# Norm application on Trainium2: the column scale moved into VectorE's multiplication, the shift on ScalarE, GpSimd taken out

## The chip, the cores and the metric

The kernel runs on one core of a Trainium2 chip. A core has five engines that work side by side from queues of their own: TensorE (PE, matrix products), VectorE (DVE), ScalarE (ACT), GpSimd (POOL) and SyncE (SP, which here starts the transfers). The metric is the device time of one execution in microseconds, from the first instruction to the last.

## The reference

Two transformer blocks of depth 2 each, on 512 tokens (the first block with 256 context tokens beside them) of width 1024, in float32. What matters here are the norms between the matrix products:

```
def rms_norm(x, g):
    y = x * lax.rsqrt(jnp.mean(x * x, axis=-1, keepdims=True) + EPS)
    return y * g
def modulate(h, shift, scale):
    return h * (1.0 + scale) + shift
def layer_norm(x, g, b):
    mu = jnp.mean(x, axis=-1, keepdims=True)
    var = jnp.mean(jnp.square(x - mu), axis=-1, keepdims=True)
    return (x - mu) * lax.rsqrt(var + LN_EPS) * g + b
```

The first block applies the RMS norm with a shift and a scale ahead of w_in and of w_up, and adds each product to the residual that was there before the norm. The second block applies the layer norm after w_mix, w_mo and w_ff2, and its result is the next residual.

## The kernel before

Activations lie with the features on the partitions: eight tiles `xs[0..7]` of 128 features by 512 tokens (768 with the context). A product in full precision is three products of rounded numbers: each weight tile and each activation is split into a rounded high part and a low part, and TensorE adds up high x high, low x high and high x low. So a norm's output is a pair: `h[:, 0]` is the rounded value, and `h[:, 1]` is the residual, the unrounded value less the rounded one.

*Weights.* A transfer brings a weight tile `wf`; ScalarE rounds it to `wh` (L241), and an engine subtracts to get `wl` (L243; the names end in x for the second of two sets of buffers). That engine is GpSimd for the matrices in `POOL_SPLIT` (w_in, w_in2, w_mix, w_out), else VectorE, unless `split_on` names another one.

*Norms.* The scale and shift are columns, one number per feature and so per partition; the deviation `r` and the mean `mu` are tiles of one number per token. For each of the eight tiles a norm does: VectorE multiplies by `r` (L294, L358, L1460); ScalarE scales, shifts and rounds to `h[:, 0]` (L298, L362, L1465); GpSimd scales and shifts without rounding (L299, L366, L1469); VectorE subtracts for the residual (L300, L367, L1471). There are three places in the code. `rms_chunks` makes the first norm of the kernel, 768 columns wide. `norm_linear` holds the RMS norms that follow a product (w_out, w_down): the last products and the norm go in two pieces of columns, 512 and 256, or 256 and 256, so that the norm of one piece goes beside the products of the other. `res_norm` with `ln_feed`, `ln_late`, `ln_stats` and `ln_apply` does the same for the layer norms, in two halves of 256 columns. There `ln_apply` first subtracts the mean (L1456, tiles 0 to 4 on VectorE and 5 to 7 on GpSimd, by `LND`), and what GpSimd makes is written back to `xs` as the next residual; ScalarE does this in its place for tiles 0 and 4 (`AFA`, L1467), and for tiles 1, 3, 5, 7 in the last norm (`AFB`), which makes no `h`.

*The head.* While a half is normed, TensorE takes each finished `h` tile at once into the first products of the next matrix (the `head`: L1487 is w_mq's, L1507 w_in2's, L1067 w_up's, L1090 w_in's, L529 those of the first norm). At the two places in `LNC` (half 0 behind tile 7, half 1 behind tile 3) `res_norm` has the next weight tile split, and with `LNP` set this is put on GpSimd whatever the matrix.

*Order.* Code is issued tile by tile; a scheduler then orders each engine's queue ahead of time, and at run time an engine takes its queue strictly in order. What VectorE or ScalarE holds ahead of a tile's `h` therefore delays it, whatever else is ready.

## Time and profile before

| | us |
|---|---|
| median of 3 runs (lowest to highest) | 3614.79 (3611.59 to 3618.96) |
| the profiled execution | 3614.98 |
| its span in the profile | 3613.2 |
| TensorE busy | 3404.7 |
| VectorE busy | 2062.0 |
| ScalarE busy | 1616.5 |
| GpSimd busy | 764.6 |

The mean granted clock of TensorE over the span is 0.979 of full speed. A timeline row gives the start, the duration, the engine, the line, the operation, what is written and read, and how many instructions of this kind stand in a row; in brackets is how long the engine was idle before, and what released it. Where several stand in one row, the duration is that of all together.

### The profile page before, as it was taken

The page shows a single profiled execution, that of the slowest core. Times are in us where ns is not written, and L with a number is a line of the kernel's source. Part 1 is how long each engine was busy: PE and PEld are TensorE (multiplying, and loading weights), DVE is VectorE, ACT ScalarE, POOL GpSimd, SP SyncE. Part 2 cuts the span into 40 slices and gives each one's busy share as a digit, 9 for nine tenths or more (in the row PEclk, how much of TensorE's full clock was granted, in tenths as well). Part 3 has the DMA queues.
Part 4 walks back from the last instruction along what each step waited for, and adds up shares of the span by engine and source line. Part 5 has one row for each costly group of instructions (what it writes and reads, how often), then busy time and mean ns, then how long its engine had stood idle before and what let it go on. Part 6 is the DMA issues. An engine that isn't in the chain of part 4 may idle for free. (4 is left out here: it accounts for less than half of the span.)

```text
span 3613.2 us, 51613 instructions
## 1 busy us (share of the span) xinstructions
PE 3404.7 (94%) x19888; PEld 2864.2 (79%) x19888; DVE 2062.0 (57%) x4037; ACT 1616.5 (45%) x3239; POOL 764.6 (21%) x706
## 2 busy tenths in 40 slices
PE   7999999999998999899999999899998989999998
PEld 5777777888887778688887777788887877888887
DVE  5765537777445764455555774664446683664444
ACT  4876624222224766543335454543224455443323
POOL 3233232000004233320002315230005314340002
PEclk9999999999999999999999999999999999999999
DMA  6111252445122010323323242323232243303331
GB/s 210 32 44 60 71 203 89 134 150 188 53 62 68 27 59 32 99 74 100 94 86 94 76 141 73 117 71 99 99 93 79 65 129 98 128 30 111 99 99 59
DMA packets 118054, 333.71 MB, mean 92 GB/s; under 512 B 18736, under 2 KB 35632, under 8 KB 117168
## 3 DMA queue, kind: packets, MB, share of 16 engines
q1 hardware_dynamic: 117808, 330.41, 28.9%
q8 instruction: 157, 2.57, 0.3%
q14 instruction: 89, 0.73, 0.1%
HBM read 313.19 MB, written 17.18 MB: 91 GB/s over the span
## 5 line engine op out<-in xcount | busy, mean ns | idle before, releaser
L241 ACT CAST wh<-wf 128x1024 fp32r<-128x1024 f32 (+1 forms) x245 | 250.2, 1022 | 555.9 <-PE M L1570 254.2
L243 DVE TENSOR_TENSOR wl<-wf,wh 128x1024 fp32r<-128x1024 f32 (+1 forms) x168 | 196.9, 1172 | 258.0 <-ACT wh L241 257.9
L496 PE MATMUL M<-wh,h 128*128 128x256 f32 x1472 | 321.7, 294 | 7.4 <-ACT t_st L565 3.0
L243 POOL TENSOR_TENSOR wl<-wf,wh 128x1024 fp32r<-128x1024 f32 x77 | 185.0, 2406 | 651.1 <-ACT wh L241 616.8
L1106 PE MATMUL S<-h,wh 128*128 128x512 f32 x1008 | 268.4, 361 | 6.2 <-DVE y L1118 5.9
L241 ACT CAST whx<-wf 128x1024 fp32r<-128x1024 f32 (+2 forms) x211 | 210.5, 998 | 137.4 <-PE M L1570 61.4
L496 PEld LDWEIGHTS M<-wh,h 128*128 128x128 f32 x1472 | 245.7, 191 | 28.4 <-issue 21.8
L1106 PE MATMUL S<-h,whx 128*128 128x512 f32 x1008 | 265.0, 358 | 0.0
L243 DVE TENSOR_TENSOR wlx<-wf,whx 128x1024 fp32r<-128x1024 f32 (+2 forms) x168 | 199.4, 1187 | 39.0 <-ACT whx L241 38.2
L496 PE MATMUL M<-wl,h 128*128 128x256 f32 x736 | 210.4, 286 | 3.3 <-POOL wl L243 3.3
L1684 PE MATMUL T<-ident,P 128*128 128x128 f32 x1136 | 186.1, 282 | 18.6 <-POOL P L1676 5.3
L1106 PEld LDWEIGHTS S<-h,wh 128*128 128x128 f32 x1008 | 168.1, 190 | 38.1 <-ACT wh L241 3.9
L1106 PEld LDWEIGHTS S<-h,whx 128*128 128x128 f32 x1008 | 165.7, 188 | 29.3
L788 ACT COPY pT<-T 128x512 f32<-128x512 f32 (+1 forms) x280 | 156.5, 569 | 58.2 <-PE T L1684 47.7
L1684 PEld LDWEIGHTS T<-ident,P 128*128 128x128 f32 x1136 | 129.6, 142 | 53.8 <-POOL P L1676 12.4
L1116 DVE SCALAR_TENSOR_TENSOR y<-S,pp,y 128x511 f32<-128x511 f32 (+1 forms) x132 | 86.6, 657 | 143.8 <-ACT y L1113 143.7
L1113 ACT ACTIVATE y<-S,pp 128x768 f32<-128x768 f32 (+1 forms) x88 | 77.8, 886 | 187.7 <-PE S L1106 181.5
L1570 PE MATMUL S<-h,wh 128*128 128x512 f32 x480 | 158.1, 390 | 0.0
L1570 PE MATMUL S<-h,whx 128*128 128x512 f32 x480 | 157.5, 389 | 0.0
L1106 PE MATMUL S<-h,wl 128*128 128x512 f32 x504 | 154.7, 361 | 0.0
L1106 PE MATMUL S<-h,wlx 128*128 128x512 f32 x504 | 152.2, 356 | 0.0
L691 PE MATMUL S<-k,q 128*128 128x512 f32 (+1 forms) x576 | 142.6, 353 | 9.1 <-ACT P L750 4.2
(518 smaller groups left out, 9215.9 us busy)
## 6 DMA issues: line engine op xcount, KB each, us to landing
wf<-in_w_ff_dram SPq DMA_DIRECT2D x128, 512.0 KB, 3.4
wf<-in_w_up_dram SPq DMA_DIRECT2D x88, 512.0 KB, 3.5
wf<-in_w_in_dram SPq DMA_DIRECT2D x80, 512.0 KB, 3.5
af<-in_adaT_dram SPq DMA_DIRECT2D x56, 512.0 KB, 4.1
wf<-in_w_down_dram SPq DMA_DIRECT2D x48, 384.0 KB, 3.1
wf<-in_w_mkv_dram SPq DMA_DIRECT2D x32, 512.0 KB, 3.6
ak<-in_adaK_dram SPq DMA_DIRECT2D x16, 512.0 KB, 9.4
wf<-in_w_out_dram SPq DMA_DIRECT2D x16, 512.0 KB, 3.6
```

The lines of the kernel that those rows point to most:

```text
L241: self.nc.scalar.copy(hi, f)
L243: eng.tensor_sub(lo, f, hi.bitcast(F32))
L496: mm = self.nc.tensor.matmul(ps[:, :256], a, c, start=(n == 0), stop=(n == 23))
L691: self.nc.tensor.matmul(ps[:, a:b], lhs, r[:, a:b], start=(i == 0), stop=(i == n - 1))
L788: nc.scalar.copy(hl[:, :w], pT[:, :w])
L1106: nc.tensor.matmul(ps[:, s0:s1], a, hs[k][:, mj, s0:s1], start=(q == 0), stop=(q == 23))
L1113: nc.scalar.activation(y[:, :n], ps[:, :n], AF.Identity, scale=col(cw + 1), bias=col(cb))
L1116: nc.vector.scalar_tensor_tensor(y[:, s0 + 1:s1], ps[:, s0:s1 - 1], col(cw), y[:, s0 + 1:s1], op0=ALU.mult, op1=ALU.add)
L1570: self.nc.tensor.matmul(ps, w[k // 4][jw][:, k % 4, c * P:(c + 1) * P], hs[k][:, jm], start=(i == 0), stop=(i == 23))
L1684: self.nc.tensor.transpose(pT[:, n * P:(n + 1) * P], pt[:, j, (kp + i) * P:(kp + i + 1) * P], self.ident)
```

## The change

In all three places VectorE's multiplication now takes the scale column as well, `(x * scale) * r`, in one three-operand instruction; ScalarE adds the shift and rounds; VectorE makes the residual as `(x + shift) - h`, again in one instruction. GpSimd has no part in it. In `rms_chunks` the 768 columns become 512 and 256 on VectorE, as the scale differs for the context. In `ln_apply` all eight mean subtractions are VectorE's, the product is written in place (the temporary tile is gone), and since `xs` must then hold x + b, ScalarE adds it for all eight tiles: after the loop where `h` is made, in the loop in the last norm. `LNP` is 0, so that the splits at the places of `LNC` are VectorE's unless the matrix is in `POOL_SPLIT`. The constants `LND`, `AFA`, `AFB` and `NAF` are gone.

```diff
-LNP = 1
+LNP = 0
@@ rms_chunks
-            nc.vector.tensor_mul(t[:, :n], xs[m][:, :n], r[:, :n])
...
-                    nc.scalar.activation(h[:, 0, a:b], t[:, a:b], AF.Identity, scale=scale(m, v), bias=shift(m, v))
-                    nc.gpsimd.tensor_scalar(t[:, a:b], t[:, a:b], scale(m, v), shift(m, v), op0=ALU.mult, op1=ALU.add)
-            nc.vector.tensor_sub(h[:, 1, :n], t[:, :n], h[:, 0, :n].bitcast(F32))
+                    nc.vector.scalar_tensor_tensor(t[:, a:b], xs[m][:, a:b], scale(m, v), r[:, a:b], op0=ALU.mult, op1=ALU.mult)
+                    nc.scalar.activation(h[:, 0, a:b], t[:, a:b], AF.Identity, bias=shift(m, v))
+                    nc.vector.scalar_tensor_tensor(h[:, 1, a:b], t[:, a:b], shift(m, v), h[:, 0, a:b].bitcast(F32),
+                                                   op0=ALU.add, op1=ALU.subtract)
@@ norm_linear
-                nc.vector.tensor_mul(t, xs[m][:, a:b], r[:, a:b])
+                nc.vector.scalar_tensor_tensor(t, xs[m][:, a:b], scale(m, v), r[:, a:b], op0=ALU.mult, op1=ALU.mult)
...
-                self.behind = nc.scalar.activation(h[:, 0, a:b], t, AF.Identity, scale=scale(m, v), bias=shift(m, v))
...
-                    nc.gpsimd.tensor_scalar(t, t, scale(m, v), shift(m, v), op0=ALU.mult, op1=ALU.add)
-                self.behind_v = nc.vector.tensor_sub(h[:, 1, a:b], t, h[:, 0, a:b].bitcast(F32))
+                self.behind = nc.scalar.activation(h[:, 0, a:b], t, AF.Identity, bias=shift(m, v))
+                self.behind_v = nc.vector.scalar_tensor_tensor(h[:, 1, a:b], t, shift(m, v), h[:, 0, a:b].bitcast(F32),
+                                                               op0=ALU.add, op1=ALU.subtract)
@@ ln_apply
-            (nc.vector if m < LND else nc.gpsimd).tensor_sub(x, x, mu)
+            nc.vector.tensor_sub(x, x, mu)
...
-            nc.vector.tensor_mul(t, x, r)
+            nc.vector.scalar_tensor_tensor(x, x, g(m), r, op0=ALU.mult, op1=ALU.mult)
...
-                self.behind = nc.scalar.activation(h[:, 0, sl], t, AF.Identity, scale=g(m), bias=b(m))
-            if m in (AFA if hs is not None else AFB):
-                nc.scalar.activation(x, t, AF.Identity, scale=g(m), bias=b(m))
+                self.behind = nc.scalar.activation(h[:, 0, sl], x, AF.Identity, bias=b(m))
+                nc.vector.scalar_tensor_tensor(h[:, 1, sl], x, b(m), h[:, 0, sl].bitcast(F32), op0=ALU.add, op1=ALU.subtract)
             else:
-                nc.gpsimd.tensor_scalar(x, t, g(m), b(m), op0=ALU.mult, op1=ALU.add)
-            if hs is not None:
-                nc.vector.tensor_sub(h[:, 1, sl], x, h[:, 0, sl].bitcast(F32))
+                nc.scalar.activation(x, x, AF.Identity, bias=b(m))
             yield m
+        for m in range(KC) if hs is not None else ():
+            nc.scalar.activation(xs[m][:, sl], xs[m][:, sl], AF.Identity, bias=b(m))
```

Where `h` is made, ScalarE writes `xs` in 20 instructions before (two in each of ten halves) and in 80 after; in the last norm in 8 before and 16 after. VectorE makes the subtractions of the mean in 60 instructions before and 96 after.

VectorE's queue at the start of half 1 of the norm after w_mix in the first layer, before. L1456 subtracts the mean, L1444 makes the variance, L1460 multiplies into the temporary `pT`, L1471 makes the residual; `x2_0` to `x2_7` are the tiles, `score2` is the mean and `score3` the deviation:

```order
L1456 TENSOR_TENSOR x2_0_18102<-x2_0_18102,score2_21278 128x256
L1471 TENSOR_TENSOR h6_21649<-x2_6_18114,h6_21649 128x256
L1444 SCALAR_TENSOR_TENSOR score3_21279<-T_21580,score3_21279 128x256
L1456 TENSOR_TENSOR x2_1_18104<-x2_1_18104,score2_21278 128x256
L1471 TENSOR_TENSOR h7_21661<-x2_7_18116,h7_21661 128x256
L1456 TENSOR_TENSOR x2_2_18106<-x2_2_18106,score2_21278 128x256
L1456 TENSOR_TENSOR x2_3_18108<-x2_3_18108,score2_21278 128x256
L1456 TENSOR_TENSOR x2_4_18110<-x2_4_18110,score2_21278 128x256
L1460 TENSOR_TENSOR pT_21685<-x2_0_18102,score3_21279 128x256
L1460 TENSOR_TENSOR pT_21696<-x2_1_18104,score3_21279 128x256
L1460 TENSOR_TENSOR pT_21707<-x2_2_18106,score3_21279 128x256
L1471 TENSOR_TENSOR h0_21500<-x2_0_18102,h0_21500 128x256
```

The same place after (L1449 subtracts, L1437 makes the variance, L1452 multiplies, L1458 makes the residual, L239 splits a weight tile):

```order
L1449 TENSOR_TENSOR x2_0_18054<-x2_0_18054,score2_21230 128x256
L1449 TENSOR_TENSOR x2_1_18056<-x2_1_18056,score2_21230 128x256
L1449 TENSOR_TENSOR x2_2_18058<-x2_2_18058,score2_21230 128x256
L239 TENSOR_TENSOR wl_21608<-wf_21249,wh_21607 128x1024
L1437 SCALAR_TENSOR_TENSOR score3_21231<-T_21526,score3_21231 128x256
L1449 TENSOR_TENSOR x2_3_18060<-x2_3_18060,score2_21230 128x256
L1449 TENSOR_TENSOR x2_4_18062<-x2_4_18062,score2_21230 128x256
L1449 TENSOR_TENSOR x2_5_18064<-x2_5_18064,score2_21230 128x256
L1449 TENSOR_TENSOR x2_6_18066<-x2_6_18066,score2_21230 128x256
L1449 TENSOR_TENSOR x2_7_18068<-x2_7_18068,score2_21230 128x256
L1452 SCALAR_TENSOR_TENSOR x2_0_18054<-x2_0_18054,pp_70,score3_21231 128x256
L1452 SCALAR_TENSOR_TENSOR x2_1_18056<-x2_1_18056,pp_70,score3_21231 128x256
```

Eight subtractions stand where five stood, the weight split stands among them where GpSimd had it, and both residuals of half 0 (h6, h7) that stood among the subtractions have moved ahead of them.

ScalarE's queue in half 0 of the same norm, before. L1465 rounds to `h`, L1467 writes `xs`, L1428 squares a tile for half 1's statistic, L1442 to L1443 begin that statistic:

```order
L1465 ACTIVATE h2_21573<-pT_21571,pp_70 128x256
L1465 ACTIVATE h3_21613<-pT_21611,pp_70 128x256
L1428 ACTIVATE P_21280<-x2_7_18116 128x256
L1465 ACTIVATE h4_21625<-pT_21623,pp_70 128x256
L1467 ACTIVATE x2_4_18110<-pT_21623,pp_70 128x256
L1465 ACTIVATE h5_21637<-pT_21635,pp_70 128x256
L1442 ACTIVATE score2_21278<-T_21580 128x256
L1465 ACTIVATE h6_21649<-pT_21647,pp_70 128x256
L1443 ACTIVATE score3_21279<-score2_21278 128x256
L1465 ACTIVATE h7_21661<-pT_21659,pp_70 128x256
```

The same place after (L1457 rounds, L1463 adds the shift to `xs`, L1421 squares, L1435 and L1436 begin the statistic, L237 rounds a weight tile):

```order
L1421 ACTIVATE pT_21490<-x2_6_18066 128x256
L1457 ACTIVATE h5_21578<-x2_5_18064,pp_70 128x256
L1463 ACTIVATE x2_0_18054<-x2_0_18054,pp_70 128x256
L1463 ACTIVATE x2_1_18056<-x2_1_18056,pp_70 128x256
L1463 ACTIVATE x2_2_18058<-x2_2_18058,pp_70 128x256
L1463 ACTIVATE x2_3_18060<-x2_3_18060,pp_70 128x256
L1421 ACTIVATE P_21232<-x2_7_18068 128x256
L1463 ACTIVATE x2_4_18062<-x2_4_18062,pp_70 128x256
L1457 ACTIVATE h6_21588<-x2_6_18066,pp_70 128x256
L1457 ACTIVATE h7_21598<-x2_7_18068,pp_70 128x256
L1435 ACTIVATE score2_21230<-T_21526 128x256
L237 CAST wh_21607<-wf_21249 128x1024
```

Five additions stand ahead of h6 and h7, four of them also ahead of the square of tile 7, and the start of half 1's statistic stands behind h7.

ScalarE's queue at the end of half 1, before, up to the extraction of q (L1379):

```order
L1465 ACTIVATE h5_21637<-pT_21746,pp_70 128x256
L1465 ACTIVATE h6_21649<-pT_21757,pp_70 128x256
L1465 ACTIVATE h7_21661<-pT_21768,pp_70 128x256
L241 CAST wh_21793<-wf_21675 128x1024
L1379 ACTIVATE q0_21787<-M_21591 128x512
```

After:

```order
L1457 ACTIVATE h6_21588<-x2_6_18066,pp_70 128x256
L1457 ACTIVATE h7_21598<-x2_7_18068,pp_70 128x256
L1463 ACTIVATE x2_3_18060<-x2_3_18060,pp_70 128x256
L237 CAST wh_21729<-wf_21611 128x1024
L1463 ACTIVATE x2_4_18062<-x2_4_18062,pp_70 128x256
L1463 ACTIVATE x2_5_18064<-x2_5_18064,pp_70 128x256
L1463 ACTIVATE x2_6_18066<-x2_6_18066,pp_70 128x256
L1463 ACTIVATE x2_7_18068<-x2_7_18068,pp_70 128x256
L1372 ACTIVATE q0_21723<-M_21537 128x512
```

Five additions stand between h7 and the extraction of q, four of them behind the rounding of the next weight tile, where before only this rounding stood there.

## Rows read from the trace of the kernel before

**Rows 1.** Page, busy us of each engine, share of the span, instructions.

```profile
PE 3404.7 (94%) x19888; PEld 2864.2 (79%) x19888; DVE 2062.0 (57%) x4037; ACT 1616.5 (45%) x3239; POOL 764.6 (21%) x706
```

**Rows 2.** Windows: stretch, length; busy us (count) PE, PEld, DVE, ACT, POOL; clock; DMA.

```profile
32.30:67.80 35.50, 29.66 (x232) 23.86 (x232) 25.23 (x43) 12.01 (x19) 20.75 (x18) 0.86 0.53 139
536.50:574.50 38.00, 33.46 (x155) 26.40 (x154) 22.22 (x39) 18.66 (x26) 19.68 (x18) 0.96 0.09 28
1117.70:1157.20 39.50, 30.42 (x177) 25.51 (x175) 27.07 (x36) 16.03 (x25) 25.40 (x21) 0.91 0.14 47
1548.00:1573.60 25.60, 21.58 (x155) 20.05 (x154) 16.94 (x39) 14.46 (x25) 15.46 (x17) 0.94 0.13 43
2250.00:2279.80 29.80, 23.76 (x170) 22.45 (x169) 26.57 (x52) 17.43 (x33) 22.26 (x22) 0.94 0.09 27
2387.50:2416.40 28.90, 25.13 (x172) 24.03 (x172) 26.61 (x52) 17.20 (x33) 23.46 (x22) 0.88 0.08 21
2750.90:2784.60 33.70, 24.65 (x170) 23.08 (x168) 28.77 (x53) 17.62 (x35) 25.71 (x23) 0.90 0.11 36
...
sum 309.40, PE 247.97 PEld 220.75 DVE 242.04 ACT 156.96 POOL 213.04; mean PE 24.80 PEld 22.08 DVE 24.20 ACT 15.70 POOL 21.30
```

**Rows 3.** Timeline: start, us, instruction, idle before and releaser; E1, after w_mix.

```profile
2263.13 0.41 DVE L1456 TENSOR_TENSOR x<-x,score 128x256 f32<-128x256 f32 x1
...
2265.35 4.32 DVE L1456 TENSOR_TENSOR x<-x,score 128x256 f32<-128x256 f32 x3
...
2266.88 2.52 POOL L243 TENSOR_TENSOR wl<-wf,wh 128x1024 fp32r<-128x1024 f32 x1
...
2270.70 0.58 PE L1487 MATMUL M<-h,wh 128*128 128x256 f32 x1 [3.65 <-ACT h L1465]
...
2275.01 2.53 POOL L243 TENSOR_TENSOR wlx<-wf,whx 128x1024 fp32r<-128x1024 f32 x1
...
2275.24 2.59 DVE L1460 TENSOR_TENSOR pT<-x,score 128x256 f32<-128x256 f32 x1
...
2278.22 0.63 PE L1487 MATMUL M<-h,whx 128*128 128x256 f32 x3 [1.84 <-DVE h L1471]
```

**Rows 4.** View of line L1456, ns shortest/median/longest.

```profile
L1456 DVE TENSOR_TENSOR x<-x,score x20: 407/792/2556, 2250.0 to 3106.1; 128x256 f32<-128x256 f32 x20
```

**Rows 5.** Timeline, first norm (A).

```profile
54.60 4.66 POOL L243 TENSOR_TENSOR wl<-wf,wh 128x1024 fp32r<-128x1024 f32 x2
...
54.66 5.41 DVE L300 TENSOR_TENSOR h<-x,h 128x768 fp32r<-128x768 f32 x1 [0.49 <-POOL x L299]
...
60.13 0.80 PE L529 MATMUL M<-wh,h 128*128 128x256 f32 x2 [3.29 <-DVE h L300]
```

**Rows 6.** Timeline, norm after w_down (C).

```profile
1127.61 2.97 DVE L367 TENSOR_TENSOR h<-x,h 128x256 fp32r<-128x256 f32 x2
...
1127.86 2.44 POOL L243 TENSOR_TENSOR wl<-wf,wh 128x1024 fp32r<-128x1024 f32 x1
...
1131.24 2.08 PE L341 MATMUL T<-r,ones 128*128 128x512 f32 x2 [4.56 <-DVE r L333]
```

**Rows 7.** Timeline, norm after w_out (B), second half.

```profile
558.14 2.50 DVE L358 TENSOR_TENSOR y<-x,sq 128x512 f32<-128x512 f32 x4 [0.57 <-ACT sq L343]
...
559.86 5.19 POOL L366 TENSOR_SCALAR y<-y,mod,mod 128x512 f32<-128x512 f32 x4 [2.75 <-ACT h L362]
```

**Rows 8.** Page, costliest groups: xcount, busy us, mean ns, idle before.

```profile
L243 DVE TENSOR_TENSOR wl<-wf,wh 128x1024 fp32r<-128x1024 f32 (+1 forms) x168 | 196.9, 1172 | 258.0 <-ACT wh L241 257.9
```

**Rows 9.** Groups of VectorE by line and shape, same columns.

```profile
L410 DVE SCALAR_TENSOR_TENSOR af<-af,sc 128x1024 f32<-128x1024 f32 x56 | 68.2, 1218 | 11.3 <-DMA af<-in_adaT_dram 11.1
```

**Rows 10.** Timeline, last norm (F).

```profile
3604.75 1.42 DVE L1460 TENSOR_TENSOR lt<-x,ln 128x256 f32<-128x256 f32 x4
3605.27 3.82 POOL L1469 TENSOR_SCALAR x<-lt,pp 128x256 f32<-128x256 f32 x4 [1.06 <-DVE lt L1460]
```

**Rows 11.** Timeline of ScalarE, norm after w_ff2 (E3).

```profile
2774.10 1.57 ACT L1465 ACTIVATE h<-lt,pp 128x256 fp32r<-128x256 f32 x3
```

More of the change, by code (lines that the diff above doesn't have):

```diff
@@ L43 @@
 STB = 4
-LND = 5
 OFF2 = 1.2
@@ L52 @@
 WX = 1
-LNP = 1
+LNP = 0
 LNC = ((0, 7), (1, 3))
-AFA = (0, 4)
-AFB = (1, 3, 5, 7)
-NAF = ()
 NC_ = ((0, 7), (1, 3))
@@ L1455, in ln_apply @@
             x = xs[m][:, sl]
-            (nc.vector if m < LND else nc.gpsimd).tensor_sub(x, x, mu)
+            nc.vector.tensor_sub(x, x, mu)
         for m in range(KC):
             x = xs[m][:, sl]
-            t = st["pool"].tile([P, 256], F32, name=st["tmp"], bufs=st["tb"])
-            nc.vector.tensor_mul(t, x, r)
+            nc.vector.scalar_tensor_tensor(x, x, g(m), r, op0=ALU.mult, op1=ALU.mult)
             if hs is not None:
```

3 lines of the change are left out of this document (removed).

## The prediction

> **What bounds the kernel now.** I began with the page's busy times: TensorE works 3404.7 us of a span of 3613.2, VectorE 2062.0, ScalarE 1616.5, GpSimd 764.6 [rows 1]. So the kernel is bound by TensorE's own work, which the change leaves alone, and all that can be had is in the 3613.2 - 3404.7 = 208.5 us in which no matmul ran. (The page's chain that ended last covers only the end of the kernel, and says nothing of the middle.) Next I cut the trace at the ten places where a norm is applied: the first norm of the kernel (A), after w_out (B, D), after w_down (C), after w_mix and w_mo in either layer (E1, E2, twice each), after w_ff2 (E3), and the last norm (F). One table of windows has them: 309.40 us in all with 247.97 us of matmuls, so 61.4 us of the idle time stands here [rows 2], in 9% of the span. VectorE is busy for 58 to 92% of these windows and GpSimd for 52 to 81%, against 57% and 21% over the whole span.
>
> Then I read the worst windows instruction by instruction. In half 1 of the norm after w_mix, GpSimd starts the split of a weight tile at 2266.88 and takes 2.52 us; three VectorE subtractions of L1456 that began at 2265.35 last 4.32 us together; TensorE starts again at 2270.70, after 3.65 us of nothing [rows 3]. By the view of that line a subtraction takes 407 ns at best, 792 in the median and 2556 at worst [rows 4]; the worst is as long as the split. The same pair comes again 8 us on: split 2.53 us at 2275.01, VectorE's multiplication 2.59 us at 2275.24, TensorE idle for 1.84 us [rows 3]. In A two splits in a row (4.66 us) stand beside one subtraction of 5.41 us, behind which TensorE idles 3.29 us [rows 5]; in C a split of 2.44 us stands beside two subtractions of 2.97 us, and TensorE idles 4.56 us [rows 6]. So what ends last in these stages is a VectorE instruction that could not run while GpSimd ran. A second, smaller brake is GpSimd's own pace: in B's second half four of its 512-wide operations take 5.19 us, 1.3 us a tile, and each residual waits for one [rows 7].
>
> The Trainium skill, "SBUF — State Buffer", section "Who interferes with whom", says that VectorE and GpSimd share a pair of ports under an exclusive lock, and that a VectorE instruction with two inputs in SBUF is held for the whole of a GpSimd instruction that reads SBUF. The durations in rows 3 to 6 agree with it; it would give the change the gains worked out below from those rows.
>
> **The change part by part.** The profiled execution took 3614.98 us, 0.2 above the median of 3614.79, so the sum goes against the profile and carries over.
>
> *VectorE.* A step keeps two VectorE instructions; the plain multiplication and subtraction become ones with a column operand. No row has exactly this form. The nearest: the three-operand form at 128x1024 takes 1218 ns [rows 9], the two-operand one at that width 1172 in the mean [rows 8], so +4%. I take 0.34 us for a 256-wide one in a row (four in 1.42 us, 1.42 less a first of 0.41, over three [rows 10]), and keep +4% of it, 0.3 us per half of 24, as the bound. In the second block's six norms VectorE gains the three of eight mean subtractions that GpSimd had: 3 x 0.34 = 1.0 us per half, and one weight split of 1.17 us [rows 8] in eight places that GpSimd did in about 2.5 [rows 3]. A half thus needs 24 x 0.34 = 8.2 us and mostly 1.2 for the split. Before, it needed 21 x 0.34 = 7.1 and lost some 2.15 (2556 less 407 ns [rows 4]) for each split that stalled it.
>
> The Trainium skill, "VectorE: DVE Perf Modes", section "Rules for kernel authors", advises to keep the number of chained VectorE operations small, since each ends in a drain. Here the count goes up from 21 to 24 per half, which by that rule speaks against the change; at the 0.34 us above, drain included, it is the 1.0 us already counted.
>
> In A 768 columns become pieces of 512 and 256, some 0.6 + 0.34 us in a row [rows 7, 10] against 0.88 for the whole (three quarters of 1172 ns [rows 8]): nothing.
>
> *GpSimd.* It loses every multiply-and-add of the norms (1.3 us each at 512 wide [rows 7], 3.82 us for four at 256 [rows 10]), its mean subtractions and eight splits. It keeps its splits for w_in, w_in2, w_out and w_mix, so in A, C and E3 a VectorE instruction can still meet one. What that costs there is unknown: from 0 to all of what A and C lose now.
>
> *ScalarE.* The rounding stays one instruction per tile (scale dropped). Where h is made, the eight values x + b that carry the residual on are now all ScalarE's, instead of two: +6 per half, ten halves, and +8 in F, 68 more. Three ScalarE instructions of 128x256 in a row take 1.57 us [rows 11], some 0.5 each: 34 us more work in all on an engine that is idle more than half the time. It is covered only where nothing urgent is queued behind. In the order, five of these additions of half 0 stand ahead of h6 and h7 (2.5 us), and in half 1 three stand ahead of h3 and five behind h7, ahead of the extraction of q. TensorE has six tiles of eight to work through by then: E1's window holds 170 matmuls in 23.76 us, 0.14 each [rows 2], so the six tiles' 36 matmuls last 5.0 us, which hides the 2.5 and h6's own 0.6. The five at the end are 2.5 us, of which the last tiles' matmuls behind h7 hide about half: 1.3 us in E1.
>
> *The stages, one by one.* E1, half 1: VectorE's first subtraction ran at 2263.13 and the last ended at 2265.35 + 4.32 = 2269.67 [rows 3]. Afterwards the residuals of half 0 all stand ahead of the first subtraction, so I let it start at 2263.8; eight subtractions (2.7), the split (1.2) and the variance (0.34) take 4.3 us, which ends at 2268.1, 1.6 us sooner, and TensorE follows as now. The second stall's 1.84 us go too (no GpSimd split there), less 1.3 for the additions ahead of q's extraction, which is late next: 1.6 + 1.8 - 1.3 = 2.1 each, 4.2 for both layers; the ends are -4 (additions fully exposed) and +12 (twice the 6.0 us of idle time in that window [rows 2]). E2: the same half without q's extraction: 3.8 us of idle time in the first layer's window [rows 2], of which the start of half 1 is most; I take half, 2.0 each, 4.0; ends -4 and +8. B: 4.5 us of idle time [rows 2]; a tile of the second half goes from 1.3 us (GpSimd) to two VectorE operations of 0.6 (four took 2.50 us [rows 7]), 1.2, and GpSimd's hand-overs between them go: 3.5 of the 4.5, and 1.5 for the granted clock of this window, which at 0.96 of 38 us stands for 1.5 us of lost clock [rows 2]; ends 0 and 6. D: 4.0 us of idle time, the same steps: 3.0 of 0 to 5. C: 9.1 us of idle time; the stall of 2.97 goes only if no split of w_in falls there, and those are still GpSimd's: 3.5 of 0 to 9. A: 5.8 us of idle time at a clock of 0.86; the 5.41 us can come again, but GpSimd has no more norm steps ahead of its splits, which so fall earlier: 4.0 of 0 to 9. E3: 9.1 us idle; its splits stay on GpSimd: 2.5 of 0 to 6. F: GpSimd's 3.82 us for four tiles [rows 10] go, but eight ScalarE additions of 0.5 each, one behind each multiplication, take 4 us: 0.5 of -1 to 1.
>
> Sum: 4.2 + 4.0 + 5.0 + 3.0 + 3.5 + 4.0 + 2.5 + 0.5 = 26.7 us. 3614.98 - 26.7 = 3588.3, and 3588.1 against the median. The rest of the kernel (GpSimd steps outside the norms) I cost at nothing, since its order moves by a few instructions only.
>
> **The rivals.** *One, VectorE becomes the bound of the norms, no change.* A half needs 8.2 us of VectorE and 1.2 for its split, 9.4, against 48 x 0.14 = 6.7 us of matmuls. If TensorE has to follow VectorE through all ten halves, E1, E2, E3 gain nothing (10.7 us of the sum), and with A and C's stalls remaining (7.5) only 8.5 are left: 3606.5. For it: VectorE is busy 89% of E1's window and 92% of E2's [rows 2]. Against it: a good part of that busy time is stalls (792 ns median against 407).
>
> *Two, ScalarE's additions stand in the way, slower.* If the 2.5 us ahead of h6 and h7 are not covered, and the 2.5 us behind h7 hold q, relu and the next weight's rounding, each of the ten halves loses up to 3.0 us more (six additions of 0.5), 30 us, against gains of 15.5 in A to D and half of 10.7 in E: 3615 + 30 - 21 = 3624. It decides from the point where the squares of x6 and x7, or h6, come later than TensorE's last ready matmul, some 5.0 us after h0. Against it: in the order x6's square stands ahead of the additions and x7's behind four, and ScalarE is busy 58% of E1's window [rows 2].
>
> *Three, all stalls go and the clock stays up.* If VectorE never meets a split again, 45 of the 61.4 us go, and the windows' granted clocks of 0.86 to 0.96 [rows 2] rise; 0.04 of 248 us of matmuls are 10 us: 3615 - 55 = 3560.
>
> *Four, the change doesn't do what it says:* if remaining GpSimd work in the norms' statistics (sum of squares) and its own splits stall as much as before, only pace is won: 3603 to 3612; it goes with rival one.
>
> **How the numbers follow.** The forecast, 3572 to 3602, has 0.60. Rivals one and four, 3602 to 3614, have 0.20, rival two, 3614 to 3635, 0.08, and rival three, 3550 to 3572, 0.12. The predicted time is 3588. The range of 3564 to 3608 leaves out some 0.05 below and 0.15 above. Within 0.2% means 3607.6 to 3622.0, which is about what a measurement of this kernel can tell from no change. Faster: 0.60 + 0.12 + 0.06 of the rivals one and four's part below 3607.6 = 0.78; same 0.15; slower 0.07.
>
> **What would show it.** Right: in the windows of rows 2 TensorE's idle time sums to 30 to 40 us; no 256-wide VectorE instruction of E1 and E2 lasts over 1 us; the gap at half 1 of E1 is under 2 us; GpSimd has 70 to 120 us less in the windows. Wrong: gaps before h6 or q that ScalarE's additions release (rival two), TensorE waiting tile by tile for VectorE's residual (rival one), or VectorE instructions of 2.5 us in A, C and E3 as before (part of rival four). The forecast falls if the six-tile cover of TensorE in half 0 is smaller than I take it, or if the column operand costs a 256-wide instruction more than the 4% of the wide one.

## The result and the profile after

The changed kernel takes 3569.64 us in the median (3565.26 to 3570.55, 4 runs) against 3616.88 before (3611.59 to 3619.73, 4 runs): 0.9869 of the time, with a 95% interval of 0.9857 to 0.9882, which is 47.2 us less. The forecast was 26.7 us less, 3588, in a range of 3564 to 3608. So the direction and the range held, but the gain is over three quarters larger than forecast, and the time lies in the band of the third rival (3550 to 3572, a chance of 0.12), not in the forecast's own (3572 to 3602).

The profiled execution took 3565.26 us, with a span of 3563.5 after 3613.2. Its busy times on the page, to be read against rows 1:

```profile
PE 3387.9 (95%) x19888; PEld 2849.7 (80%) x19888; DVE 2049.9 (58%) x4097; ACT 1626.3 (46%) x3307; POOL 590.8 (17%) x530
```

TensorE's matmuls, the same 19888, are 3404.7 - 3387.9 = 16.8 us shorter, and its idle time went from 208.5 to 3563.5 - 3387.9 = 175.6 us, 32.9 less. Together that is the 49.7 us of the span. So a third of the gain is not idle time at all: the same matmuls ran at a higher granted clock, 0.984 in the mean over the span after 0.979.

The windows of the norms, from the same matmul to the same matmul as in rows 2 (stretch, length, then busy us and count of TensorE, its weight loads, VectorE, ScalarE, GpSimd, and the granted clock as the third number from the end):

```profile
32.14:62.56 30.42, 28.58 (x232) 22.23 (x233) 22.54 (x47) 10.77 (x18) 4.73 (x3) 0.93 0.53 161
532.43:563.43 31.00, 31.00 (x155) 25.40 (x154) 22.14 (x37) 15.02 (x24) 1.60 (x2) 1.00 0.11 35
1108.15:1135.53 27.38, 26.86 (x177) 23.80 (x176) 22.35 (x36) 14.92 (x24) 11.61 (x5) 1.00 0.15 52
1524.18:1544.58 20.40, 19.61 (x156) 18.70 (x154) 16.90 (x38) 11.44 (x24) 0.74 (x1) 1.00 0.13 35
2220.30:2245.86 25.56, 22.93 (x170) 21.20 (x169) 25.32 (x60) 19.41 (x45) 1.81 (x2) 1.00 0.16 54
2353.15:2377.98 24.83, 23.27 (x172) 21.79 (x171) 24.56 (x60) 18.59 (x43) 1.80 (x2) 1.00 0.09 29
2711.94:2739.44 27.50, 22.88 (x171) 21.24 (x170) 26.52 (x61) 19.82 (x47) 6.89 (x4) 1.00 0.14 44
...
sum 256.69, PE 232.04 PEld 207.09 DVE 226.26 ACT 159.31 POOL 34.56; mean PE 23.20 PEld 20.71 DVE 22.63 ACT 15.93 POOL 3.46
```

Against rows 2 the ten windows went from 309.40 to 256.69 us, TensorE's busy time in them from 247.97 to 232.04, its idle time from 61.4 to 24.7, and GpSimd's busy time from 213 to 34.6 us. The granted clock, 0.86 to 0.96 in those rows before, is 1.00 in all those shown here but A (F, left out here as in rows 2, is cut by time). VectorE, however, is now busy 25.32 us of E1's 25.56. In the timeline of half 1 of E1, VectorE's and TensorE's rows show what is left of the gaps of 3.65 and 1.84 us in rows 3:

```profile
2233.27 1.09 DVE L1449 TENSOR_TENSOR x<-x,score 128x256 f32<-128x256 f32 x3
...
2234.28 1.22 DVE L239 TENSOR_TENSOR wl<-wf,wh 128x1024 fp32r<-128x1024 f32 x1
...
2235.75 1.76 DVE L1449 TENSOR_TENSOR x<-x,score 128x256 f32<-128x256 f32 x5
...
2237.42 1.27 DVE L1452 SCALAR_TENSOR_TENSOR x<-x,pp,score 128x256 f32<-128x256 f32 x3
...
2238.50 0.39 PE L1478 MATMUL M<-h,wh 128*128 128x256 f32 x1 [1.05 <-ACT h L1457]
...
2238.61 1.27 DVE L1458 SCALAR_TENSOR_TENSOR h<-x,pp,h 128x256 fp32r<-128x256 f32 x3
...
2242.18 1.22 DVE L239 TENSOR_TENSOR wlx<-wf,whx 128x1024 fp32r<-128x1024 f32 x1
...
2243.85 0.62 PE L1478 MATMUL M<-h,whx 128*128 128x256 f32 x3 [0.86 <-DVE h L1458]
```

In E1 no VectorE instruction stands for 2.5 us any more; VectorE goes from one to the next without a pause. The gap at the start of the half is 1.05 us: it ends when ScalarE has rounded the first tile, which waited for the multiplications, which stood behind eight subtractions and the split of 1.22 us. The second gap, 0.86 us, stands behind the other split. E3, where the splits are still GpSimd's, keeps the old picture: a split beside five VectorE subtractions of 3.98 us, and another beside four residuals of 3.72 us and a gap of 2.07:

```profile
2725.77 2.47 POOL L239 TENSOR_TENSOR wl<-wf,wh 128x1024 fp32r<-128x1024 f32 x1 [7.02 <-ACT wh L237]
2725.89 3.98 DVE L1449 TENSOR_TENSOR x<-x,ln 128x256 f32<-128x256 f32 x5
...
2734.22 2.62 POOL L239 TENSOR_TENSOR wlx<-wf,whx 128x1024 fp32r<-128x1024 f32 x1 [5.98 <-ACT whx L237]
...
2734.59 3.72 DVE L1458 SCALAR_TENSOR_TENSOR h<-x,pp,h 128x256 fp32r<-128x256 f32 x4
...
2737.18 0.51 PE L1498 MATMUL S<-whx,h 128*128 128x256 f32 x2 [2.07 <-DVE h L1458]
```

In C, two splits of GpSimd still run beside the norm, but there GpSimd is held first (compare rows 6, where a split took 2.44 us and VectorE stood). The last row is the view of the two splits (shortest, median and longest, in ns):

```profile
1128.40 8.60 POOL L239 TENSOR_TENSOR wl<-wf,wh 128x1024 fp32r<-128x1024 f32 x2 [7.56 <-ACT wh L237]
...
1129.19 2.07 DVE L359 SCALAR_TENSOR_TENSOR h<-x,mod,h 128x512 fp32r<-128x512 f32 x3
...
1131.18 0.74 DVE L354 SCALAR_TENSOR_TENSOR x<-x,mod,sq 128x512 f32<-128x512 f32 x1
...
1132.87 1.87 DVE L359 SCALAR_TENSOR_TENSOR h<-x,mod,h 128x512 fp32r<-128x512 f32 x1 [0.94 <-ACT h L358]
...
L239 POOL TENSOR_TENSOR wl<-wf,wh x2: 2843/4315/5787, 1128.4 to 1134.2; 128x1024 fp32r<-128x1024 f32 x2
```

The first split takes 5.79 us where one took 2.44 (5.78 to 5.80 in this kernel and in seven of those below), while three of VectorE's 512-wide instructions beside it take 2.07 together, as fast as anywhere. VectorE pauses at 1131.92. The split ends 2.27 us later, at 1134.19, about as long as a split takes that meets nothing, and now VectorE's next instruction stands, 1.87 us instead of 0.74. The second split takes 2.84. So in C the first split waited until VectorE paused, and then held VectorE. A queue of VectorE without pauses does not explain this alone: VectorE makes no pause ahead of the splits of E3 either, and there they start at once (2.47 and 2.62 us) and VectorE stands. What decides between the two is not shown.

One warning for all that follows. The windows repeat: B takes 30.9 to 31.1 us in every run with the changed norms, D 20.4 (20.9 in ones_scale, which alters its code), E1 25.5 to 25.6 in all that leave its code alone. Other stretches don't: from the end of E3 to a matmul some 380 further on, the time is 64.5, 67.4 and 71.5 us in three profiles (splits_dve, best_b and the changed kernel) with the same code there, at granted clocks of 0.64 to 0.85 in the four parts of it in the changed kernel, and A takes 28.8 to 31.8 us with the same code. Times of one kernel lie some 5 to 15 us apart. So differences under some 5 us are read from the windows, and times serve for the large ones.

### The profile page after: what moved, and what is told of

Read it like the earlier page. It is cut to its first block, busy times and chain, and to the rows that moved or that the text cites. A ratio compares the mean times of both kernels' runs of the same rounds, so it can differ in the third digit from the quotient of the medians.

```text
span 3563.5 us, 51437 instructions
## 1 busy us (share of the span) xinstructions
PE 3387.9 (95%) x19888; PEld 2849.7 (80%) x19888; DVE 2049.9 (58%) x4097; ACT 1626.3 (46%) x3307; POOL 590.8 (17%) x530
## 4 chain that ended last, share of the span: by engine, by line
PE 76%; DVE 12%; ACT 5%; POOL 3%; issue 2%; DMA 1%; SPq 0%; ACTq 0%; POOLq 0%; DVEq 0%
PE S L1099 17%; PE M L1561 14%; PE S L1561 9%; PE M L1037 7%; PE M L489 6%; PE M L769 4%; PE T L1675 3%; PE M L1517 2%; PE S L684 2%; PE T L1039 2%; PE M L1611 2%; PE M L319 2%; PE T L570 1%; PE M L1338 1%; DVE score L1646 1%
## 5 line engine op out<-in xcount | busy, mean ns | idle before, releaser
L237 ACT CAST wh<-wf 128x1024 fp32r<-128x1024 f32 (+1 forms) x245 | 250.2, 1022 | 550.7 <-PE M L1561 256.4
L239 DVE TENSOR_TENSOR wl<-wf,wh 128x1024 fp32r<-128x1024 f32 (+1 forms) x172 | 201.9, 1174 | 253.4 <-ACT wh L237 253.4
L239 POOL TENSOR_TENSOR wl<-wf,wh 128x1024 fp32r<-128x1024 f32 x73 | 178.7, 2452 | 715.8 <-ACT wh L237 683.0
L237 ACT CAST whx<-wf 128x1024 fp32r<-128x1024 f32 (+2 forms) x211 | 210.4, 998 | 138.1 <-PE M L1561 61.4
L239 DVE TENSOR_TENSOR wlx<-wf,whx 128x1024 fp32r<-128x1024 f32 (+2 forms) x172 | 204.3, 1188 | 43.8 <-ACT whx L237 43.1
```

The costliest lines, as they stand in the source:

```text
L237: self.nc.scalar.copy(hi, f)
L239: eng.tensor_sub(lo, f, hi.bitcast(F32))
```

## Experiments

The theories: 1, a running GpSimd instruction that reads SBUF holds a VectorE instruction with two inputs there, and what VectorE lost in this way is what was won; 2, what was won is the step through GpSimd in the chain; 3, ScalarE's added work takes part of it back. The length of the windows, in us, each from the start of the same matmul to the start of the same matmul, F to the end of the span:

```
               A    B    C    D    E1   E2   E3   E1'  E2'  F
before        35.5 37.8 39.6 25.7 29.8 28.9 33.7 29.6 29.0 23.7
changed       30.4 31.0 27.4 20.4 25.6 24.8 27.5 25.4 25.2 22.5
splits_only   35.5 37.1 39.3 25.7 27.6 27.1 33.6 27.5 27.4 23.4
splits_back   30.3 31.0 27.3 20.4 27.6 27.4 27.5 27.5 27.7 22.1
rms_only      30.3 31.0 27.4 20.4 29.7 28.6 32.5 29.6 29.0 23.4
ln_only       35.4 37.4 39.3 25.1 27.7 27.3 29.0 28.9 27.7 22.1
shadow_read   29.1 31.0 27.4 20.4 27.5 26.9 29.4 27.4 27.0 22.1
shadow_set    31.8 31.0 27.3 20.4 25.6 24.8 27.2 25.4 25.2 22.1
splits_dve    30.5 31.0 28.7 20.4 25.5 24.8 25.4 25.4 25.2 22.1
ones_scale    27.6 31.1 32.2 20.9 25.9 25.1 27.8 25.7 25.4 22.6
no_adds       28.8 31.1 27.4 20.4 25.2 24.6 29.3 25.1 25.2 22.4
scalar_twice  35.7 33.0 29.0 23.6 29.7 28.5 33.6 29.6 29.0 23.4
best_a        28.9 31.0 27.4 20.4 25.5 24.8 25.4 25.4 25.2 22.5
best_b        30.3 30.9 27.4 20.4 24.4 24.5 24.3 24.3 24.6 22.5
```

### The change in its parts

**The splits alone** (splits_only), the kernel before with

```diff
-LNP = 1
+LNP = 0
```

> The kernel before with one part of the change alone: the eight weight splits at the places of LNC go from GpSimd to VectorE (LNP 0). Theory 1 (a running GpSimd instruction holds a VectorE instruction with two inputs in SBUF): the 2.5 us VectorE instructions of the norms after w_mix and w_mo go, TensorE's gaps of 3.65 and 1.84 us at half 1 shrink by some 2 us each, 2 to 3 us are won at each of the four norms, 8 to 12 us in all: 3605 to 3609 against 3616.9. Theory 2 (what held TensorE was the chain's step on GpSimd, not the splits): the chain keeps that step, and VectorE has 1.2 us more per half: 0 to 2 us won, 3615 to 3617.

Measured: 3613.67 us, a ratio of 1.0000 [0.9988, 1.0011]. Its windows E1 to E2' are 1.6 to 2.2 us shorter, at or a little under the 2 to 3 of theory 1, but the median shows nothing of these 7.7 us: by the time alone, theory 2's figure was met. About 1 us each of E1 and E1' is given back behind the window (the stretch up to the next window took 108.8 us after 107.7, and 108.4 after 107.3); the rest is lost among stretches that vary by more. In E1 TensorE's two gaps are

```profile
2266.62 1.75 DVE L243 TENSOR_TENSOR wl<-wf,wh 128x1024 fp32r<-128x1024 f32 x1
...
2270.07 0.58 PE L1487 MATMUL M<-h,wh 128*128 128x256 f32 x1 [2.62 <-ACT h L1465]
...
2275.45 0.62 PE L1487 MATMUL M<-h,whx 128*128 128x256 f32 x3 [0.27 <-DVE h L1471]
```

2.62 us instead of 3.65 and 0.27 instead of 1.84, but the split on VectorE itself now takes 1.75 us beside GpSimd's mean subtractions. GpSimd stays in the chain, and so moving the splits alone is worth 7.7 us in the windows and nothing that the time shows.

**The splits back** (splits_back), the changed kernel with

```diff
-LNP = 0
+LNP = 1
```

> The changed kernel with the eight splits put back on GpSimd (LNP 1). Theory 1: VectorE instructions of some 2.5 us return in the norms after w_mix and w_mo, 8 to 12 us are lost against the changed kernel's 3569.6: 3577 to 3582. Theory 2: GpSimd has nothing in the chain now and does the splits beside it, and VectorE has 1.2 us less per half: 3566 to 3571.

Measured: 3574.34 us, 0.9887 [0.9863, 0.9911], 4.7 us over the changed kernel by the medians, though the intervals overlap. The windows decide: E1, E2, E1', E2' are 2.0 to 2.6 us longer each, 9.2 together, and all others within 0.4. The long instruction is back in the line's view (shortest, median, longest ns):

```profile
L1449 DVE TENSOR_TENSOR x<-x,score x32: 405/419/2636, 2220.2 to 3072.8; 128x256 f32<-128x256 f32 x32
```

where the changed kernel has

```profile
L1449 DVE TENSOR_TENSOR x<-x,score x32: 415/419/426, 2220.3 to 3066.1; 128x256 f32<-128x256 f32 x32
```

So theory 1 holds for the splits, by the windows and at the lower end of what it said; the time, 3574.34, falls between the two expectations.

**The first block's norms alone** (rms_only), the kernel before with the changed rms_chunks and norm_linear:

```diff
-                nc.vector.tensor_mul(t, xs[m][:, a:b], r[:, a:b])
+                nc.vector.scalar_tensor_tensor(t, xs[m][:, a:b], scale(m, v), r[:, a:b], op0=ALU.mult, op1=ALU.mult)
...
```

> The kernel before with the changed rms_chunks and norm_linear alone, that is the first block's norms (A to D). From the two traces these stages are shorter by 5.1 + 6.8 + 12.2 + 5.3 = 29.4 us, of which some 4 are given back right behind A and B: if the stages are independent, 25 to 28 us are won: 3589 to 3592. If part of these gains hangs on the second block's part (order, clock), under 20 us: over 3597.

Measured: 3582.0 us, 0.9910 [0.9895, 0.9926], 31.8 us less: more than expected. Its windows A to D are those of the changed kernel to 0.1 us, and E1 to F those of before to 0.3, but for 1.2 us in E3. The stages are independent, and four norms of the first block give two thirds of the gain by the times, and 29.5 of 53.2 us by the windows.

**The second block's norms alone** (ln_only), the kernel before with the changed ln_apply, LNP still 1:

```diff
-            (nc.vector if m < LND else nc.gpsimd).tensor_sub(x, x, mu)
+            nc.vector.tensor_sub(x, x, mu)
...
-                nc.gpsimd.tensor_scalar(x, t, g(m), b(m), op0=ALU.mult, op1=ALU.add)
```

> The kernel before with the changed ln_apply alone (second block, E1 to F), the eight splits still on GpSimd. From the two traces these stages are shorter by 23.7 us with the splits moved. Theory 1: without the moved splits VectorE still stands for 2.5 us at half 1 of E1 and E2, so 10 to 15 us are won: 3602 to 3607. Theory 2: nearly all of it, 20 to 24 us: 3593 to 3597.

Measured: 3605.09 us, 0.9973 [0.9961, 0.9985], 8.7 us less; its windows E1 to F are 2.1, 1.6, 4.7, 0.7, 1.3 and 1.7 us shorter, 12.1 together, theory 1's figure. With its splits moved as well (the changed kernel) the six windows win 23.8 us: 12.1 for this part, 7.7 for the splits alone, and 4.0 only where both come together.

### What held VectorE

**GpSimd busy beside the norm, out of the chain** (shadow_read), the changed kernel with

```diff
                 self.behind = nc.scalar.activation(h[:, 0, sl], x, AF.Identity, bias=b(m))
+                gd = self.hp.tile([P, 256], F32, name="gd", bufs=1)
+                nc.gpsimd.tensor_scalar(gd[:, :256], h[:, 0, sl].bitcast(F32), g(m), g(m), op0=ALU.mult, op1=ALU.add)
```

> The changed kernel, and GpSimd does again one 256-wide multiply-and-add per tile in ln_apply where h is made, from h[:, 0] into a tile that nothing reads, so it holds up nothing by a dependence. VectorE's queue is the same, row by row. Theory 1 (a GpSimd instruction that reads SBUF and a VectorE instruction with two SBUF inputs hold each other): VectorE's 256-wide instructions of E1 to E3, 0.42 and 0.48 us in the median now, rise to 0.55 or more in the mean, and the five windows E1 to E2' get longer by 1 to 3 us each, 5 to 15 us in all: 3575 to 3585. Theory 2 (only the step through GpSimd in the chain cost time): windows within 0.3 us of the changed kernel's, 3568 to 3572.

**GpSimd as busy, without reading** (shadow_set), with

```diff
+                gd = self.hp.tile([P, 256], F32, name="gd", bufs=1)
+                for _ in range(3):
+                    gm = nc.gpsimd.memset(gd, 0.0)
+                    self.tc.add_manual_dep(gm.ins, self.behind.ins.name, SYNC, reason="shadow")
```

> As the run before, but with three memsets of 128x256 per tile, released by the same rounding instruction, in place of the multiply-and-add: GpSimd is as busy, and reads nothing. Theory 1 in its narrow form (only GpSimd instructions that read SBUF hold VectorE): windows and VectorE's durations as in the changed kernel, within 0.3 us. If any GpSimd instruction holds VectorE: 5 to 15 us more, as with the reading one. Theory 2: no difference either way.

Measured: 3576.64 us, 0.9897 [0.9876, 0.9918], with the reading instructions, and 3564.79, 0.9863 [0.9848, 0.9878], with the memsets. With reading, E1 to E2' are 1.8 to 2.1 us longer than in the changed kernel, 9.6 us in the five; with memsets all five are within 0.3. The groups by line and shape (count, busy us, mean ns), first the changed kernel's residual on VectorE and ScalarE's rounding, then GpSimd's reading instruction and VectorE's residual beside it, then memset and residual:

```profile
L1458 DVE SCALAR_TENSOR_TENSOR h<-x,pp,h 128x256 fp32r<-128x256 f32 x80 | 37.1, 503 | 1.2 <-ACT h L1457 1.2
...
L1457 ACT ACTIVATE h<-x,pp 128x256 fp32r<-128x256 f32 x80 | 35.6, 498 | 12.7 <-DVE x L1452 10.4 <-PE M L1517 2.4
```

```profile
L1459 POOL TENSOR_SCALAR gd<-h,pp 128x256 f32<-128x256 f32 x80 | 79.1, 989 | 36.8 <-ACT h L1457 30.5
...
L1460 DVE SCALAR_TENSOR_TENSOR h<-x,pp,h 128x256 fp32r<-128x256 f32 x80 | 41.1, 552 | 1.1 <-ACT h L1457 1.1
```

```profile
L1460 POOL MEMSET gd<- 128x256 f32 x240 | 74.9, 312 | 32.1 <-ACT h L1457 19.1
...
L1462 DVE SCALAR_TENSOR_TENSOR h<-x,pp,h 128x256 fp32r<-128x256 f32 x80 | 37.6, 508 | 1.2 <-ACT h L1457 1.2
```

GpSimd is as long busy in both, 79.1 and 74.9 us, and VectorE's queue is the same, row by row. Nothing waits for what GpSimd makes here, yet reading costs 1.9 us per norm. So the hold of theory 1 is shown, in its narrow form: it is the reading of SBUF. VectorE's durations rose less than expected: this residual from 503 to 552 ns, the subtractions and multiplications of the norm by 3 to 23 ns; with one more instruction of the statistics that is some 7 us of VectorE's time, of the 9.6 lost. GpSimd's own instruction takes 989 ns, against 549 at the shortest in the kernel before, so much of the conflict falls on GpSimd. The Trainium skill, "SBUF — State Buffer", section "Who interferes with whom", limits the hold to GpSimd instructions that read SBUF; these two runs agree.

**GpSimd out of the chain by other means** (scalar_twice), the kernel before with

```diff
-NAF = ()
+NAF = (0, 1, 2, 3, 4, 5, 6, 7)
```

> The kernel before with norm_linear's unrounded value on ScalarE for all eight tiles (NAF), so GpSimd is out of B, C and D, but VectorE's instructions stay the two-operand ones and ScalarE makes two values per tile at some 0.5 to 0.7 us each. If GpSimd's leaving is what gained (hold and step): C, where one VectorE instruction stood 2.6 us, gets 4 to 9 us shorter, B and D, paced at 1.3 us per tile by GpSimd and now at 1.4 by ScalarE, are within 1 us of before. If the three-operand form itself (two instructions per tile with nothing between but the rounding) is what gained: C within 1 us of before too, or longer.

Measured: 3600.81 us, 0.9952 [0.9938, 0.9966], 16.0 us less. C is 10.6 us shorter of the changed kernel's 12.2, B 4.8 of 6.8, D 2.1 of 5.3. So in B, C and D most of the gain, 17.5 of 24.3 us, comes with GpSimd's leaving by other means too; the expectation for C was too low, and those for B and D as well. A split of 2.37 us still runs in C, but VectorE has a pause of 3.6 us there and so meets nothing, and the gap near it is 0.59 us (rows 6 had 4.56):

```profile
1128.08 2.37 POOL L243 TENSOR_TENSOR wl<-wf,wh 128x1024 fp32r<-128x1024 f32 x1 [5.09 <-ACT wh L241]
...
1128.59 1.13 PE L341 MATMUL T<-sq,ones 128*128 128x512 f32 x2 [0.59 <-ACT sq L331]
```

Hold and step are not taken apart by this run: both go. In B and D of the kernel before no VectorE instruction lasts over 1.25 us, so what was won there is not the long hold of rows 3 to 6; the step and pace of GpSimd [rows 7] are what is left of the two theories.

**The remaining splits** (splits_dve), the changed kernel with

```diff
-                    self.split_on = nc.gpsimd if LNP else None
+                    self.split_on = nc.vector
...
                 if (p, m) in NC_:
+                    self.split_on = nc.vector
                     with self.tc.issue_after(self.behind.ins):
                         self.wsplit_upto(self.wsplit + 1)
+                    self.split_on = None
```

> The changed kernel with the four splits that stayed on GpSimd beside norms (two of w_in in C, two of w_in2 in E3) on VectorE as well. Theory 1: in E3 the VectorE instructions of 2.6 us and the gap of 2.07 us before whx go, for 1.2 us more of VectorE each: E3 1 to 3 us shorter; C has 0.5 us of idle time left and gains 0 to 0.5; 3566 to 3569. Rival: VectorE is full in E3 (26.5 of 27.5 us), so its two added splits cost what the stalls cost: E3 within 0.5 us, 3569 to 3571.

Measured: 3561.24 us, 0.9853 [0.9838, 0.9868], less than either expectation gave, by more than its windows explain. E3 is 2.1 us shorter, as theory 1 said. C is 1.3 us longer, which neither said: VectorE has the splits' 1.2 us in its queue, and a gap is new,

```profile
1136.67 0.51 PE L1085 MATMUL M<-whx,h 128*128 128x256 f32 x2 [1.04 <-DVE h L359]
```

So the same move is right in E3, where GpSimd's split held VectorE, and wrong in C, where the split of GpSimd waited for VectorE (5.79 us) and its result was not yet needed.

### ScalarE

**A scale column put back** (ones_scale), the changed kernel with

```diff
-                self.behind = nc.scalar.activation(h[:, 0, sl], x, AF.Identity, bias=b(m))
+                self.behind = nc.scalar.activation(h[:, 0, sl], x, AF.Identity, scale=self.ones[:, 0:1], bias=b(m))
```

and the same in the other roundings and, other than the expectation says, in the additions after the loop as well.

> The changed kernel with a column of ones as scale in ScalarE's instructions of the norms (the two roundings, and x + b in the last norm; the additions after the loop stay without it). It tells whether the 0.50 us of such an instruction at 128x256, against 0.59 before, comes from the scale column that the change took away, and whether ScalarE's time counts. If the column is the cause: 0.59 us again. If ScalarE is near the path in half 1 (16 instructions of it per half), E1 to E3 lose 0.3 to 1 us each; if it has slack, windows within 0.2 us.

Measured: 3571.97 us, 0.9884 [0.9868, 0.9901]. The rounding takes

```profile
L1457 ACT ACTIVATE h<-x,pp,ones 128x256 fp32r<-128x256 f32 x80 | 43.5, 591 | 10.9 <-DVE x L1452 8.2 <-PE M L1517 2.4
```

591 ns against 498 in the changed kernel (above): the column costs 93 ns per instruction, and the change takes it away. The Trainium skill, "ScalarE: Activation LUTs", section "What ACT_TABLE_LOAD costs", gives some 93 ns for each operand that is a column; the runs agree. E1 to E2' lose 0.2 to 0.3 us each, the low end of the expectation. C loses 4.8 us, which was not expected. By the trace it is an order: the scheduler put VectorE's queue in C in another order, and a GpSimd split now stands beside the addition of the statistics on which TensorE waits,

```profile
1109.62 2.39 POOL L239 TENSOR_TENSOR wl<-wf,wh 128x1024 fp32r<-128x1024 f32 x1 [2.33 <-ACT wh L237]
1110.17 2.39 DVE L329 TENSOR_TENSOR r<-r,y 128x512 f32<-128x512 f32 x1 [0.36 <-ACT y L327]
...
1112.61 1.18 PE L337 MATMUL T<-r,ones 128*128 128x512 f32 x2 [2.97 <-DVE r L329]
```

So C's good result in the changed kernel hangs on where a split of GpSimd happens to fall; the other runs with the changed norms have it in the good place (splits_dve has the later two on VectorE).

**The additions left out** (no_adds), without

```diff
-        for m in range(KC) if hs is not None else ():
-            nc.scalar.activation(xs[m][:, sl], xs[m][:, sl], AF.Identity, bias=b(m))
```

> The changed kernel without ScalarE's 80 additions x + b after the loop of ln_apply: the shift is left out of the residual that is carried on, so the result is not the reference's. It prices what the second rival of the prediction rests on. If the additions are covered (ScalarE has slack): the windows E1 to E2' are within 0.3 us of the changed kernel's each. By my own costing (1.3 us behind h7 ahead of q in E1, 0.2 to 0.5 ahead of h6): E1 and E1' 1.5 to 2 us shorter, E2, E2', E3 0.3 to 1. By the rival: up to 3 us per half, 6 per window.

Measured: 3567.46 us, 0.9861 [0.9848, 0.9875]. E1, E2, E1', E2' are 0.3, 0.3, 0.3 and 0.0 us shorter; E3 came out 1.8 us longer: the order there changed too, and two GpSimd splits instead of one now stand beside the last four residuals, which take 5.82 us instead of 3.72; the window's clock is 0.94 instead of 1.00. In E1 the gaps are

```profile
2238.61 0.39 PE L1476 MATMUL M<-h,wh 128*128 128x256 f32 x1 [1.06 <-ACT h L1457]
...
2243.59 0.62 PE L1476 MATMUL M<-h,whx 128*128 128x256 f32 x3 [0.51 <-DVE h L1458]
...
2248.24 0.50 PE L1559 MATMUL M<-h,wh 128*128 128x512 f32 x1 [1.43 <-DVE q L1373]
```

1.06 us at the start of the half, as in the changed kernel, and 1.43 us ahead of the first matmul that waits for q, where the changed kernel has

```profile
2247.61 0.50 PE L1561 MATMUL M<-h,wh 128*128 128x512 f32 x1 [1.11 <-DVE q L1373]
```

and the kernel before

```profile
2282.04 0.50 PE L1570 MATMUL M<-h,wh 128*128 128x512 f32 x1 [1.47 <-DVE q L1380]
```

The gap ahead of q is no shorter without the additions, and with them it is shorter than before the change. The comparison with no_adds is not quite clean, as a weight split stands ahead of VectorE's last residual there and behind it in the changed kernel. The 0.3 us per window are all that the additions can be seen to cost: they are covered but for that, and theory 3 falls.

### Two versions

**The splits of E3 on VectorE, those of C on GpSimd** (best_a), the changed kernel with

```diff
-                    self.split_on = nc.gpsimd if LNP else None
+                    self.split_on = nc.vector
```

> The changed kernel with only the two splits of w_in2 in E3 on VectorE; those of w_in in C, which cost 1.3 us there when moved, stay on GpSimd. Expected from the windows: E3 2.1 us shorter, all others as in the changed kernel, about 2 us in all, 3560 to 3568; a difference to the changed kernel that times alone can hardly tell.

**And the splits later** (best_b), best_a with

```diff
-LNC = ((0, 7), (1, 3))
+LNC = ((1, 3), (1, 7))
```

> As best_a, and the two splits beside the layer norms are issued later: behind tiles 3 and 7 of half 1 instead of behind tile 7 of half 0 and tile 3 of half 1. If the split ahead of half 1's multiplications is what leaves the gap of 1.05 us at the start of half 1: the gap goes, E1, E2, E1', E2' each 0.8 to 1.2 us shorter. If VectorE is the bound through the whole half (24 instructions and the splits): the wait moves to the end of half 1 or to the next matrix, windows within 0.3 us or longer.

Measured: best_a 3565.61 us, 0.9853 [0.9839, 0.9866]; best_b 3561.64, 0.9849 [0.9835, 0.9862]. best_a does what was expected, E3 25.4 and all else as it was, but for A, which varies. In best_b E1 and E1' are 1.1 us shorter than in best_a and E3 too, E2 and E2' 0.3 and 0.6. The gap of 1.05 us at the start of the half is gone (the first row has no idle time ahead of it), and the gap later in the half is as long as it was:

```profile
2241.41 0.39 PE L1478 MATMUL M<-h,wh 128*128 128x256 f32 x1
...
2246.76 0.62 PE L1478 MATMUL M<-h,whx 128*128 128x256 f32 x3 [0.86 <-DVE h L1458]
```

So the split ahead of the half did leave that gap, and VectorE's fullness gives none of it back in E1, some of it in E2. Against the changed kernel best_b wins 6.3 us in the windows (253.8 against 260.1) and 8.0 in the medians; the intervals of both ratios overlap, so by times alone it is not established as faster than the changed kernel.

## Why the prediction held, and where it was too small

- **The place** was right. The prediction put the gain into the ten windows; they are 52.7 us shorter where the span is 49.7, so 3 us are given back elsewhere (5.5 in the stretch behind E3, where the clock differs from run to run, against some 2 won in others).
- **The mechanism** was right where it was tested, in the second block: VectorE held by reading GpSimd instructions. splits_back prices the hold of the eight splits at 9.2 us, and shadow_read a 256-wide reading instruction per tile at 1.9 us per norm; shadow_set shows that a GpSimd that doesn't read costs nothing. In the first block's norms, over half of the gain by the windows, hold and step were not taken apart; for B and D the prediction's second brake, GpSimd's pace, is the likelier.
- **The clock was the term that was mis-sized most.** The sum had 1.5 us for it, in B alone; the ten windows' matmuls became 247.97 - 232.04 = 15.9 us shorter. The third rival had 10 us for this, as part of a case of 0.12, and its 3560 is nearer to the result than the forecast's 3588. The step that failed is the first: that TensorE's own work is left alone and all that can be had is the idle time. The clock of rows 2, 0.86 to 0.96, was the sum's to use in every window: the windows whose gaps went run at 1.00. That the gaps' going is the cause is read from this, and was not made a run of its own. The kept traces bear it out only in part: E1 with 4.7 us of idle time ran at 1.00 in splits_back, and with 3.5 us at 0.94 in splits_only; A with 1.9 us ran at 0.89 in shadow_set, and with 2.1 us at 1.00 in best_a. So the idle time of a window does not by itself give its clock.
- **C was the stage most in error**, 12.2 us where 3.5 was forecast (9.2 of idle time went to 0.5, and the clock from 0.91 to 1.00). The step was "goes only if no split of w_in falls there, and those are still GpSimd's". The splits do fall there, but the first of the later two waits for VectorE, 5.79 us, and holds a single instruction of it at the end (1.87 us instead of 0.74). scalar_twice, with GpSimd out of the steps, also wins 10.6 there. What the prediction left out is that the hold has two sides. Which side is held is not forecast by pauses alone, as E3 shows, so C's gain has luck in it, and ones_scale shows it without: 4.8 us less, when a split falls in front of the statistics.
- **E1 and E2** won 4.2 and 4.0 us each, where 2.1 and 2.0 were forecast. The 1.3 us in E1 for additions ahead of q was wrong: with them q's gap is 1.11 us, after 1.47 before the change. The gap at half 1 went from 3.65 to 1.05 us, where the sum had 3.65 - 1.6 = 2.05.
- **E3**: 6.2 us against 2.5. The stalls that the prediction let stand are there (a gap of 2.07 us behind one of them), and 4.6 us of the 9.1 of idle time remain; the clock went from 0.90 to 1.00. **A, B, D and F**: 5.1, 6.8, 5.3 and 1.3 against 4.0, 5.0, 3.0 and 0.5.
- **Prices.** A three-operand 256-wide instruction on VectorE takes 478 ns (the first row below, median), not 407 to 419 plus 4%: 59 ns more, 0.9 us per half of 16. The 4% came from two rows that don't bear on it: the 1172 ns of rows 8 is a mean of two widths (the second row below has the 1024 columns alone, 1223), and the instruction of rows 9 has the constant 1.0 as its scalar and no column. A nearer row stood in the same view as rows 9, 256 wide and with a column, though with one input in PSUM (TensorE's result memory): 475 ns (the third row). ScalarE's rounding got 93 ns cheaper, which the prediction didn't see at all: ScalarE's busy time rose by 9.8 us, where 34 were forecast.

```profile
L1452 DVE SCALAR_TENSOR_TENSOR x<-x,pp,score x32: 470/478/964, 2223.3 to 3070.8; 128x256 f32<-128x256 f32 x32
...
L243 DVE TENSOR_TENSOR wl<-wf,wh 128x1024 fp32r<-128x1024 f32 x136 | 166.4, 1223 | 228.4 <-ACT wh L241 228.3
...
L1007 DVE SCALAR_TENSOR_TENSOR x<-T,mod,x 128x256 f32<-128x256 f32 x32 | 15.2, 475 | 0.0
```

- **Rival one** (VectorE the bound) is half right: VectorE is busy 25.32 of 25.56 us in E1, and best_b, which only moves a split out of its way, wins 1.1 us. But the window is 4.2 us shorter all the same, since VectorE's work is now work and not waiting. **Rival two** (ScalarE) fell by no_adds. **Rival three** had the right direction: 36.7 us of idle time went where it had 45, and 15.9 us by the clock where it had 10; but its condition, that VectorE never meets a split again, did not come true. **Rival four** fell: GpSimd's remaining splits stall VectorE in few places only.
- **The signs named beforehand**: the idle time in the windows is 24.7 us, under the 30 to 40; no VectorE instruction of 256 columns in E1 and E2 lasts over 1 us; the gap at half 1 of E1 is under 2 us; VectorE instructions of 2.5 us stayed in E3 alone (2.63 and 2.54), with one of 2.19 us beside a split in A and one of 1.87 in C. GpSimd lost 178 us in the windows, not 70 to 120, a plain miscount: rows 2 has it at 213.

Not settled: why splits_only's time shows nothing of the 7.7 us that its windows win, what sets the clock in the stretch behind E3, how hold and step share the gain of the first block, and why a split waits in C and starts at once in E3.
